# Differential keys and queries split straight out of PSUM, and a list scheduler that does not book the shared port ahead

## The chip, the core and the metric

The kernel runs on one core of a Trainium2 chip. The metric is device time in microseconds of one execution. A core has five engines that run in order and meet by semaphores: TensorE (PE; its weight loads are listed apart as PEld), VectorE (DVE), ScalarE (ACT), GpSimd (POOL) and SyncE (SP), which here issues all DMA transfers. TensorE reads SBUF and writes PSUM; POOL works in SBUF only.

## The reference

One decoder layer, sequence 512, model width 1024, all float32. Two attention branches share one input projection; the change touches the first.

```python
h = rmsnorm(x, ln_mix_g)
dq, dk, dv, nq, kc, vc, ksl, vsl, kwn, vwn, ng, mg = split(h @ w_in)
# differential attention: 8 heads, each with two query/key components c of 64, values of 128
dq, dk = rope(rmsnorm(dq)), rope(rmsnorm(dk))
s = einsum('bqhcd,bkhcd->bhcqk', dq, dk) * 64 ** -0.5
p = softmax(causal(s));  a = p[:, :, 0] - lam * p[:, :, 1]
y_diff = rmsnorm(a @ dv, subln_g) * (1 - lambda_init)
# sparse attention (NSA): 16 query heads, 4 key groups: compressed, selected and window branch
y_nsa = nsa_attention(...)
x = x + (sig(mg0) * (y_diff @ w_proj_diff) + sig(mg1) * (y_nsa @ w_proj_nsa)) @ w_out
x = x + relu(rmsnorm(x) @ w_mlp_up) ** 2 @ w_mlp_down
```

## The kernel before

Float32 products are made of rounded parts. Each operand is split into a high part (the value rounded to the matmul's format) and a low part (the rest): `split` makes a cast on ACT or DVE and a subtraction on DVE, or, for weights, on DVE or POOL. A projection is then three matmuls (high x high, high x low, low x high). Weights come in 157 pieces of up to 512 KB (`WStream`): wraw is the raw piece, whi and wlo its parts, each made in two halves of 512 columns, ahead of use.

The program goes through these stages: the norm of x and its transposes (hTh, hTl); the chunks of the input projection in four PSUM banks gb; beside them, as side streams, rope on the projected rows (`rope_stream`: t1r and t2r are its products, rw the roped rows), scores and softmax (`score_stream`), and probability times values (`value_stream`); the two output projections, merged by gates (tm, big) and w_out; and the MLP. The side streams end with the merge, some 650 to 725 us into the span. The first 77 weight pieces are used up before it.

Roped rows are transposed by TensorE into a PSUM bank ptp, one of two banks that all transposes share: keys (dk) or queries (dq) of one differential head, components 0 and 1 on the lower and the upper 64 partitions. `q_stacks` makes of a query bank two tiles of 128 partitions, qa and qb: high part on one half, low part on the other. `k_dups` makes of a key bank the tile kp (high and low, one buffer), and four DMAs copy it into kk, so that each component's parts lie on both halves. `scores` needs two matmuls then: query stack times doubled high keys, query stack times doubled low keys. The NSA keys (nk) go through `k_dups` as well. Tags: kk has 3 buffers, q has 9.

The order of all work is made before the launch. `Pe` interleaves the streams by an estimate of TensorE's time, and every instruction is noted with its priority, which is its place there (15 places ahead for the side streams). `Sched.flush` then makes a list schedule over ACT, DVE, POOL, PE and SP with prices per instruction (`price`), delays between engines and buffer counts, and issues the instructions in order of their start. Some instructions may go to either of two engines. `ported` says which instructions need the SBUF port that DVE and POOL are taken to share; self.port is the time until which it is taken. Before, an instruction under 64 elements needs none, and an engine that finds only port users ready books the one of highest priority from self.port on.

All instructions are recorded by one helper (line 357), so tiles tell them apart, not lines.

Of the kernel before, what the change touches and what calls it, by code (L numbers as in the profile page):

```python
# [11 lines left out]
F32 = mybir.dt.float32  # L12
# [119 lines left out]
class Sched:  # L132
# [34 lines left out]
    def price(self, eng, method, aps, k):  # L167
        if "accum_out" in k:
            aps = [x for x in aps if x is not k["accum_out"]]
        n = max(self.size(x) for x in aps)  # L170
        psum = any(self.tiles[x.tensor.name].space == "PSUM" for x in aps if x.tensor.name in self.tiles)
        if eng == "PE":
            if method == "transpose":
                return 113.0
            return max(113.0, 5.5 + self.size(aps[-1]) * 0.4315)
        if eng == "ACT":
            return (51 if psum else 93) + n * 0.8333 + (93 if "accum_out" in k else 0) + (
                93 if any(self.size(x) == 1 for x in aps[1:]) and n > 1 else 0)
        if eng == "DVE":
            ptr = sum(1 for x in aps[1:] if self.size(x) == 1) if n > 1 else 0  # L180
            if method in ("tensor_scalar", "tensor_copy") and not psum:
                return 69 + n * 0.52 + 61 * ptr
            if method == "memset":
                return 8 + n * 1.04
            if method == "reciprocal":
                return 69 + n * 6.25
            return 69 + n * 1.042 + 61 * ptr
        if eng == "POOL":
            if k.get("op") == OP.pow:
                return 300 + n * 165.0  # L190
            return 150 + n * 2.1
        return 20.0
# [2 lines left out]

    def ported(self, eng, method, aps, k):

        if max(self.size(x) for x in aps) < 64:
            return False
        if eng == "POOL":  # L200
            return k.get("op") != OP.pow
        return eng == "DVE" and method in self.TWICE and not any(
            self.tiles[x.tensor.name].space == "PSUM" for x in aps if x.tensor.name in self.tiles)

# [67 lines left out]
    def flush(self):  # L272

        ops, self.ops = self.ops, []
        self.wait = {e: [] for e in self.free}
        ok = {e: [] for e in self.free}
        fresh, again = [], set()
        for op in ops:
            for b in op.bufs:
                if b.group is None or b in again:  # L280
                    continue
                again.add(b)
                if b.granted:
                    self.held[b.group] += 1
                else:
                    fresh.append(b)
        for b in fresh:
            self.held.setdefault(b.group, 0)
            self.queue.setdefault(b.group, []).append(b)
        for op in ops:  # L290
            op.left, op.ready = 1, 0.0
            for d in op.deps:
                if d.left == -1:
                    op.ready = max(op.ready, d.end + self.lat(d.eng, op.eng, op.deps[d]))
                else:
                    d.users.append(op)
                    op.left += 1
            for b in op.bufs:
                if not b.granted:
                    b.waiting.append(op)  # L300
                    op.left += 1
        for g in list(self.queue):
            self.grant(g, 0.0)
        for op in ops:
            self.arm(op)
        done = []
        while len(done) < len(ops):
            best = None
            for e in self.free:
                for h, k in ((self.wait[e], 2), (ok[e], 1)):  # L310
                    while h and h[0][k].left == -1:
                        heapq.heappop(h)
                t = self.free[e] if ok[e] else max(self.free[e], self.wait[e][0][0]) if self.wait[e] else None
                if t is not None and (best is None or t < best[0]):
                    best = (t, e)
            assert best is not None, "no instruction can go on"
            t, e = best
            while self.wait[e] and self.wait[e][0][0] <= t:
                _, p, op = heapq.heappop(self.wait[e])
                if op.left == 0:  # L320
                    heapq.heappush(ok[e], (p, op))
            p, op = heapq.heappop(ok[e])
            if op.port[e] and self.port > t:
                put_off = [(p, op)]
                while ok[e] and put_off[-1][1].port[e]:
                    z = heapq.heappop(ok[e])
                    if z[1].left == 0:
                        put_off.append(z)
                if not put_off[-1][1].port[e]:
                    p, op = put_off.pop()  # L330
                else:
                    p, op = put_off.pop(0)
                for z in put_off:
                    heapq.heappush(ok[e], z)
            op.eng = e
            op.start = max(t, self.port) if op.port[e] else t
            op.end = op.start + op.ways[e][1]
            if op.port[e]:
                self.port = op.end
            self.free[e] = op.end  # L340
            if op.dma:
                self.hw = max(op.end, self.hw) + op.dma[0]
                self.dma = max(self.hw + 650, self.dma) + op.dma[1]
                op.end = self.dma
            op.left = -1
            done.append(op)
            for u in op.users:
                u.ready = max(u.ready, op.end + self.lat(e, u.eng, u.deps[op]))
                self.arm(u)
            for b in op.bufs:  # L350
                b.left -= 1
                b.end = max(b.end, op.end)
                if b.left == 0 and b.group is not None:
                    self.held[b.group] -= 1
                    self.grant(b.group, b.end + 150)
        for op in sorted(done, key=lambda o: o.start):
            op.ways[op.eng][0](*op.a, **op.k)  # L357
            op.ways = op.a = op.k = op.users = op.deps = None
# [68 lines left out]
def hybrid_block(ctx: ExitStack, tc: tile.TileContext, x, ln_mix_g, w_in, dqg, dkg, lq1, lk1, lq2, lk2,  # L427
# [137 lines left out]
    with ExitStack() as ps:  # L565
# [312 lines left out]
        def q_stacks(pt):  # L878
# [5 lines left out]
            V.tensor_tensor(qb[0:64], pt[64:128], f(qb[64:128]), op=OP.subtract)  # L884
            return qa, qb

        group_keys = {}

        def k_dups(pt, key):

            kp = att.tile([128, 2, 512], F32R, tag="kp", bufs=1, name="kp")
            split(kp[:, 0, :], kp[:, 1, :], pt)
            if key[0] == "dk":
                kk = k_tile()
                dst = [kk[:, s] for s in range(2)]
            else:

                if key[2] == 0:
                    for s in range(2):
                        group_keys[key[1], s] = k_tile()  # L900
                dst = [group_keys[key[1], s][:, key[2]] for s in range(2)]
            for s in range(2):
                for d in range(2):
                    Q.dma_start(f(dst[s][d * 64:(d + 1) * 64]), f(kp[s * 64:(s + 1) * 64]))
            return dst

        jobs = []
# [1 line left out]
        def rope_stream():  # L909

            for _ in range(8):
# [5 lines left out]
                yield 3000  # L917
                for c0, what, key in pairs:
                    sl = k_slots if what == "k" else q_slots
                    n = 2 if what == "q" else 1 if key[0] == "dk" else 2 - 2 * key[2]  # L920
                    yield sl.can(n)
                    yield t_bank()
                    sl.take(n)
                    pt = tpair(raws, c0)
                    ready[key] = there(key)
                    ready[key].tiles = k_dups(pt, key) if what == "k" else q_stacks(pt)
                    ready[key].after(6500 if what == "k" else 3500)
                    t_use(2000 if what == "k" else 3000)
                    yield 0
                r_slots.give(4)  # L930

# [93 lines left out]
        def scores(q, kk, i):  # L1025
# [3 lines left out]
                mm(sb[:, :n], q[:, i * 128:(i + 1) * 128], kk[:, z, :n], n, z == 0, z == 1)  # L1029
            return sb  # L1030

        def softmax_num(sb, i, stat):

            n = (i + 1) * 128
# [15 lines left out]
        def score_stream():  # L1050
            for h in range(8):
                yield there(("dk", h))
                yield there(("dq", h))
                kv, qv = ready["dk", h].tiles, ready["dq", h].tiles
                for i in reversed(range(NT)):
                    st = att.tile([128, 12], F32, tag="sm", bufs=8, name="sm")
                    n = (i + 1) * 128
# [2 lines left out]
                    ps_ = []  # L1060
                    for z in range(2):
                        yield s_bank()
                        ps_.append(softmax_num(scores(qv[z], kv[z], i), i, st[:, 2 * z:2 * z + 2]))
                        s_use(S_LAT + n)
                        yield 0
                    p0, p1 = ps_
# [4 lines left out]
                    probs["d", h, i] = p0  # L1071
                    stats[h, i] = st
                    there(("pd", h, i)).after(P_LAT + 3 * n)
                q_slots.give(2)
                k_slots.give(1)
            for p in range(2):
                for b in range(2):
# [571 lines left out]
```

## Time and profile before

| | |
|---|---|
| median of 3 runs | 1096.49 us (1095.57 to 1099.45) |
| the profiled execution | 1096.69 us, its span 1094.9 us |
| PE busy | 1053.8 us, 96% |
| DVE busy | 766.2 us, 70% |
| ACT busy | 465.6 us, 43% |
| POOL busy | 477.0 us, 44% |
| kk<-kp, the copies of the keys | 48 DMAs of 256 KB, 4.5 us to landing |

Matmuls are pipelined, so PE counts as busy also where it is slowed; a row's duration of a matmul is longer than the step from one to the next. A share of busy time is a mean over all stages, which have different limits. In a timeline the bracket behind a row gives the engine's idle time before it and what ended that. A wait for several semaphores is put down to the one that came last.

### The profile page before, as it was taken

The page shows a single profiled execution, that of the slowest core. Times are in us where ns is not written, and L with a number is a line of the kernel's source. Part 1 is how long each engine was busy: PE and PEld are TensorE (multiplying, and loading weights), DVE is VectorE, ACT ScalarE, POOL GpSimd, SP SyncE. Part 2 cuts the span into 40 slices and gives each one's busy share as a digit, 9 for nine tenths or more (in the row PEclk, how much of TensorE's full clock was granted, in tenths as well). Part 3 has the DMA queues.
Part 4 walks back from the last instruction along what each step waited for, and adds up shares of the span by engine and source line. Part 5 has one row for each costly group of instructions (what it writes and reads, how often), then busy time and mean ns, then how long its engine had stood idle before and what let it go on. Part 6 is the DMA issues. An engine that isn't in the chain of part 4 may idle for free.

```text
span 1094.9 us, 15737 instructions
## 1 busy us (share of the span) xinstructions
PE 1053.8 (96%) x5257; PEld 875.6 (80%) x5257; DVE 766.2 (70%) x1905; ACT 465.6 (43%) x1136; POOL 477.0 (44%) x475
## 2 busy tenths in 40 slices
PE   6999988899999999999999998999999999999998
PEld 5877867788787888887788886788888888888886
DVE  6779678899988999999989898556533323354232
ACT  4257335656464466665456563214222111242110
POOL 3745698348767372292212024423333222333221
PEclk9999988999999999999999999999999999999999
DMA  6362534642654224536363255622322223332232
GB/s 209 97 173 63 153 102 120 163 132 71 172 143 142 64 78 137 142 125 214 129 193 112 92 161 170 208 85 94 96 97 97 97 96 96 97 97 96 97 136 75
DMA packets 83616, 134.66 MB, mean 123 GB/s; under 512 B 8784, under 2 KB 33872, under 8 KB 83536
## 3 DMA queue, kind: packets, MB, share of 16 engines
q1 hardware_dynamic: 83536, 133.67, 39.7%
q8 instruction: 41, 0.67, 0.3%
q14 instruction: 39, 0.32, 0.1%
HBM read 106.64 MB, written 14.42 MB: 111 GB/s over the span
## 4 chain that ended last, share of the span: by engine, by line
PE 74%; DVE 12%; DMA 6%; POOL 4%; issue 2%; SPq 1%; ACT 1%; DVEq 0%; POOLq 0%; ACTq 0%
PE gb L357 38%; PE ga L357 22%; PE sb L357 4%; PE avn L357 4%; PE ptn L357 3%; DMA kk<-kp 3%; DVE p L357 2%; POOL str L357 1%; PE av L357 1%; POOL wlo L357 1%; SPq L357 1%; POOL t1r L357 1%; DVE al L357 1%; DVE sm L357 1%; DMA kk<-in_x_dram 1%
## 5 line engine op out<-in xcount | busy, mean ns | idle before, releaser
L357 POOL TENSOR_TENSOR wlo<-wraw,whi 128x512 fp32r<-128x512 f32 x203 | 289.0, 1432 | 522.7 <-ACT whi L357 396.2
L357 ACT CAST whi<-wraw 128x512 fp32r<-128x512 f32 (+2 forms) x217 | 130.0, 618 | 343.7 <-PE gb L357 167.0
L357 DVE CAST whi<-wraw 128x512 fp32r<-128x512 f32 x97 | 47.5, 489 | 199.7 <-PE ga L357 95.8
L357 PE MATMUL gb<-wlo,hTh 128*128 128x512 f32 (+2 forms) x352 | 136.0, 388 | 4.4 <-POOL wlo L357 2.4
L357 PE MATMUL gb<-whi,hTl 128*128 128x512 f32 (+2 forms) x352 | 135.0, 384 | 0.0
L357 PE MATMUL gb<-whi,hTh 128*128 128x512 f32 (+2 forms) x352 | 133.4, 388 | 1.5 <-ACT hTh L357 1.3
L357 DVE CUSTOM_DVE_ANT_0 p<-sb,cst 128x512 f32<-128x512 f32 (+2 forms) x192 | 92.1, 481 | 13.1 <-PE sb L357 11.7
L357 DVE TENSOR_TENSOR wlo<-wraw,whi 128x512 fp32r<-128x512 f32 (+1 forms) x111 | 92.2, 832 | 7.2 <-ACT whi L357 2.7
L357 ACT ACTIVATE p<-p,smn 128x512 f32<-128x512 f32 (+3 forms) x128 | 72.0, 563 | 26.6 <-DVE smn L357 26.2
L357 PEld LDWEIGHTS gb<-wlo,hTh 128*128 128x128 f32 x352 | 67.7, 192 | 14.8 <-POOL wlo L357 3.4
L357 PEld LDWEIGHTS gb<-whi,hTh 128*128 128x128 f32 x352 | 66.7, 191 | 11.5 <-ACT hTh L357 1.7
L357 PEld LDWEIGHTS gb<-whi,hTl 128*128 128x128 f32 x352 | 67.6, 192 | 10.3 <-DVE hTl L357 0.3
L357 DVE TENSOR_SCALAR p<-p,smn,gates 128x512 f32<-128x512 f32 (+3 forms) x128 | 66.9, 527 | 1.0
L357 PE MATMUL gb<-big,whi 128*128 128x512 f32 x192 | 65.1, 403 | 0.0
L357 PE MATMUL gb<-hTl,whi 128*128 128x512 f32 x160 | 64.7, 404 | 0.0
L357 PE MATMUL gb<-hTh,wlo 128*128 128x512 f32 x160 | 64.5, 403 | 0.0
L357 PE MATMUL gb<-hTh,whi 128*128 128x512 f32 x160 | 64.0, 400 | 0.0
L357 DVE TENSOR_TENSOR al<-ptn,ah 128x128 fp32r<-128x128 f32 (+3 forms) x128 | 61.3, 482 | 3.6 <-ACT ah L357 2.0
L357 PE MATMUL ga<-h2l,whi 128*128 128x512 f32 x160 | 62.5, 391 | 0.0
L357 PE MATMUL ga<-h2h,whi 128*128 128x512 f32 x160 | 62.4, 391 | 0.0
L357 PE MATMUL ga<-h2h,wlo 128*128 128x512 f32 x160 | 62.3, 390 | 0.0
L357 ACT CAST ah<-ptn 128x384 fp32r<-128x384 f32 (+3 forms) x98 | 41.2, 424 | 49.1 <-PE ptn L357 38.1
(248 smaller groups left out, 2634.7 us busy)
## 6 DMA issues: line engine op xcount, KB each, us to landing
wraw<-in_w_in_dram SPq DMA_DIRECT2D x36, 512.0 KB, 3.6
wraw<-in_w_mlp_up_dram SPq DMA_DIRECT2D x32, 512.0 KB, 3.8
wraw<-in_w_mlp_down_dram SPq DMA_DIRECT2D x32, 512.0 KB, 3.5
kk<-kp SPq DMA_DIRECT2D x48, 256.0 KB, 4.5
wraw<-in_w_in_dram SPq DMA_DIRECT2D x36, 256.0 KB, 3.2
big<-yd SPq DMA_DIRECT2D x16, 512.0 KB, 3.4
yd<-yo SPq DMA_DIRECT2D x8, 512.0 KB, 3.3
wraw<-in_w_proj_diff_dram SPq DMA_DIRECT2D x8, 512.0 KB, 4.3
```

What stands on the lines that cost most here:

```text
L357: op.ways[op.eng][0](*op.a, **op.k)
```

## The change

For the differential heads, `dk_stacks` writes each key component's high part to its own half and its low part to the other half, straight out of PSUM. `dq_stacks` writes the queries' high parts to both halves of the same kk tile, and the low parts to a tile ql, each component on its own half. `diff_scores` takes two matmuls: the query's high part on both halves times high and low keys (128 partitions), and the query's low part times the high keys (64 partitions). The product of both low parts is left out. `k_dups`, now for NSA keys alone, splits into the own half and copies it to the other by one DMA for each component. kp is gone; a differential head takes one q buffer for two.

In the scheduler, DVE instructions under 64 elements count as port users too; a one-column scalar_tensor_tensor costs more in `price`; and an engine that finds only port users ready, with the port taken, issues none and looks again when the port is free or its next instruction is ready.

```diff
         if eng == "DVE":
-            ptr = sum(1 for x in aps[1:] if self.size(x) == 1) if n > 1 else 0
+            ptr = sum(1 for x in aps[1:] if self.size(x) == 1) if n > 1 else method == "scalar_tensor_tensor"
...
     def ported(self, eng, method, aps, k):
-        if max(self.size(x) for x in aps) < 64:
-            return False
         if eng == "POOL":
-            return k.get("op") != OP.pow
+            return k.get("op") != OP.pow and max(self.size(x) for x in aps) >= 64
         return eng == "DVE" and method in self.TWICE and not any(
...
-                if not put_off[-1][1].port[e]:
+                go = not put_off[-1][1].port[e]
+                if go:
                     p, op = put_off.pop()
-                else:
-                    p, op = put_off.pop(0)
                 for z in put_off:
                     heapq.heappush(ok[e], z)
+                if not go:
+                    self.free[e] = min(self.port, self.wait[e][0][0]) if self.wait[e] else self.port
+                    continue
             op.eng = e
-            op.start = max(t, self.port) if op.port[e] else t
+            op.start = t
...
+        def dk_stacks(pt):
+            kt = k_tile().rearrange("p a b n -> p (a b) n")
+            for s in range(2):
+                own, other = slice(s * 64, s * 64 + 64), slice(64 - s * 64, 128 - s * 64)
+                copy(kt[own, s], pt[own])
+                V.tensor_tensor(kt[other, s], pt[own], f(kt[own, s]), op=OP.subtract)
+            return kt
+
+        def dq_stacks(pt, kt):
+            ql = att.tile([128, 512], F32R, tag="q", bufs=9, name="ql")
+            for s in range(2):
+                own, other = slice(s * 64, s * 64 + 64), slice(64 - s * 64, 128 - s * 64)
+                copy(kt[own, 2 + s], pt[own])
+                A.copy(kt[other, 2 + s], pt[own])
+                V.tensor_tensor(ql[own], pt[own], f(kt[own, 2 + s]), op=OP.subtract)
+            return ql
...
         def k_dups(pt, key):
-            kp = att.tile([128, 2, 512], F32R, tag="kp", bufs=1, name="kp")
-            split(kp[:, 0, :], kp[:, 1, :], pt)
...
             for s in range(2):
-                for d in range(2):
-                    Q.dma_start(f(dst[s][d * 64:(d + 1) * 64]), f(kp[s * 64:(s + 1) * 64]))
+                own, other = slice(s * 64, s * 64 + 64), slice(64 - s * 64, 128 - s * 64)
+                split(dst[s][own, 0], dst[s][own, 1], pt[own])
+                Q.dma_start(f(dst[s][other]), f(dst[s][own]))
...
+        def diff_scores(kt, ql, z, i):
+            n = (i + 1) * 128
+            own = slice(z * 64, z * 64 + 64)
+            sb = pscore.tile([128, 512], F32, tag="s", name="sb")
+            mm(sb[:, :n], kt[:, 2 + z, i * 128:(i + 1) * 128], kt[:, z, :n], n, True, False)
+            mm(sb[:, :n], ql[own, i * 128:(i + 1) * 128], kt[own, z, :n], n, False, True)
+            return sb
...
-                        ps_.append(softmax_num(scores(qv[z], kv[z], i), i, st[:, 2 * z:2 * z + 2]))
+                        ps_.append(softmax_num(diff_scores(kt, ql, z, i), i, st[:, 2 * z:2 * z + 2]))
```

The streams' estimate of when a key is ready changes with it: 3500 ns after its transposes for differential keys, which was 6500, and 6500 still for NSA keys.

What the scheduler makes of it is seen in the order of the built programs. The first place is DVE's row in the projection of differential heads 4 and 5, around 188 to 200 us of the trace of before; ptp is the transposed bank, sb a score bank, sm statistics, ISA p,sm the score maximum. Before, the cast into kp stands behind four DMA queues (DMAHW):

```order
L357 TENSOR_TENSOR qa_515<-ptp_514,qa_515 64x512 [waits PE_49,Activation_49]
L357 TENSOR_TENSOR qb_516<-ptp_514,qb_516 64x512
L357 RECIPROCAL sm_519<-sm_519 128x4 [waits Activation_49]
L357 TENSOR_SCALAR ys_358<-yt_541,sm_466 128x128 [waits Pool_49]
L357 SCALAR_TENSOR_TENSOR sm_519<-sm_519,lam_149 128x1 [waits DVE_49]
L357 ISA p_544,sm_533<-sb_543,cst_129 128x384 [waits PE_49]
L357 ISA sm_533 128x1
L357 SCALAR_TENSOR_TENSOR p_524<-p_532,sm_519,p_524 128x512 [waits DVE_49]
L357 CAST kp_521<-ptp_520 128x512 [waits DMAHW3_49,DMAHW4_49,DMAHW2_49,DMAHW1_49]
L357 ISA p_556,sm_533<-sb_555,cst_129 128x384 [waits PE_49]
L357 ISA sm_533 128x1
L357 TENSOR_TENSOR kp_521<-ptp_520,kp_521 128x512 [waits DVE_49]
```

The same heads in the changed program:

```order
L357 CAST kk_515<-ptp_514 64x512 [waits PE_49]
L357 ISA p_522,sm_520<-sb_521,cst_129 128x384 [waits PE_49]
L357 ISA sm_520 128x1
L357 TENSOR_TENSOR kk_515<-ptp_514,kk_515 64x512 [waits DVE_49]
L357 RECIPROCAL sm_508<-sm_508 128x4 [waits Activation_49]
L357 TENSOR_TENSOR yt_537<-yt_537,av_536 128x128 [waits Activation_49]
L357 ISA p_528,sm_520<-sb_527,cst_129 128x384 [waits PE_49]
L357 ISA sm_520 128x1
L357 CAST kk_515<-ptp_514 64x512
L357 COPY hs_575<-hb_496 128x130 [waits PE_49]
L357 TENSOR_TENSOR kk_515<-ptp_514,kk_515 64x512 [waits DVE_49]
```

The DMA queues are gone from the waits, and one head's key takes four instructions out of its bank where it took two.

The second place is DVE's row in the merge, around 664 to 672 us of before; tm are the gated sums, kk here their split, big the NSA output's split. Before:

```order
L357 TENSOR_TENSOR big_1027<-yp_1990,big_1027 128x512 [waits Activation_49]
L357 SCALAR_TENSOR_TENSOR tm_2051<-tm_2051,gb_1978 128x512 [waits DMAHW3_49,PE_49]
L357 SCALAR_TENSOR_TENSOR tm_2054<-tm_2054,gb_1979 128x512 [waits DMAHW0_49,PE_49]
L357 CAST whi_2047<-wraw_2036 128x512 [waits DMAHW1_49,PE_49,Pool_49]
L357 TENSOR_TENSOR tm_2055<-tm_2055,tm_2054 128x512 [waits DMAHW7_49,DMAHW3_49,DVE_49]
L357 SCALAR_TENSOR_TENSOR kk_2053<-tm_2052,kk_2053 128x512 [waits Activation_49]
L357 SCALAR_TENSOR_TENSOR kk_2053<-tm_2055,kk_2053 128x512 [waits Activation_49]
```

In the changed program:

```order
L357 TENSOR_TENSOR big_1009<-yp_1970,big_1009 128x512 [waits Activation_49]
L357 SCALAR_TENSOR_TENSOR tm_2031<-tm_2031,gb_1958 128x512 [waits DMAHW4_49,PE_49]
L357 TENSOR_TENSOR big_1009<-yr_2030,big_1009 128x512 [waits DMAHW5_49,Activation_49]
L357 TENSOR_TENSOR tm_2032<-tm_2032,tm_2031 128x512 [waits DMAHW1_49,DVE_49]
L357 CAST whi_2027<-wraw_2016 128x512 [waits DMAHW1_49,PE_49]
L357 SCALAR_TENSOR_TENSOR tm_2034<-tm_2034,gb_1959 128x512 [waits DMAHW7_49,DMAHW3_49]
L357 TENSOR_TENSOR wlo_2028<-wraw_2016,whi_2027 128x512 [waits PE_49,Activation_49]
L357 SCALAR_TENSOR_TENSOR kk_2033<-tm_2032,kk_2033 128x512 [waits Activation_49]
```

DVE now makes the first sum tm<-tm itself, which POOL made before, and a wlo between. Over the merge DVE makes 7 of the 8 such sums, where it made 3.

The third place is PE's row at one of the first score pairs, among matmuls of the projection (gb). Before:

```order
L357 MATMUL gb_244<-hTh_68,whi_218 128x512
L357 MATMUL sb_228<-kk_214,qa_216 128x512 [waits DMAHW3_49,DMAHW2_49]
L357 MATMUL sb_228<-kk_214,qa_216 128x512
L357 MATMUL gb_244<-hTl_69,whi_218 128x512
L357 MATMUL gb_244<-hTh_68,wlo_219 128x512
```

In the changed program, where the second of the pair is the one on 64 partitions:

```order
L357 MATMUL gb_243<-hTl_69,whi_216 128x512
L357 MATMUL sb_251<-kk_213 128x384 [waits DVE_49]
L357 MATMUL sb_251<-kk_213,ql_215 128x384
L357 MATMUL gb_243<-hTh_68,wlo_217 128x512
L357 MATMUL gb_244<-hTh_68,whi_216 128x512
```

There are 64 such matmuls from ql, and no two of them stand next to each other.

## Rows read from the trace of the kernel before

**Rows 1.** Windows by stage: busy us (instructions) per engine, granted clock, DMA, GB/s.

```profile
28.00:150.00 122.00, 119.78 (x603) 99.66 (x604) 93.98 (x223) 58.02 (x143) 77.83 (x83) 1.00 0.40 113
150.00:210.00 60.00, 50.13 (x249) 40.65 (x247) 49.20 (x120) 31.49 (x78) 39.30 (x46) 0.86 0.57 149
210.00:650.00 440.00, 429.31 (x2394) 361.77 (x2393) 408.17 (x1197) 260.21 (x708) 206.72 (x241) 1.00 0.44 132
650.00:725.00 75.00, 69.88 (x306) 56.10 (x305) 49.73 (x69) 22.26 (x40) 30.12 (x19) 0.98 0.48 162
725.00:1094.90 369.90, 366.02 (x1629) 302.54 (x1628) 145.49 (x249) 80.28 (x142) 114.07 (x74) 1.00 0.30 97
sum 1094.90, PE 1053.82 PEld 875.65 DVE 766.17 ACT 465.57 POOL 476.97; mean PE 175.64 PEld 145.94 DVE 127.70 ACT 77.60 POOL 79.49
```

**Rows 2.** Chain of waits, the MLP: start us, us, what.

```profile
873.43 43.52 PE ga L357 x192
```

**Rows 3.** Waits on the copies of kp: us in total, times, longest us.

```profile
ACT kp L357 <- DMA kk<-kp: 5.7, 3, 2.1
DVE kp L357 <- DMA kk<-kp: 5.7, 3, 2.8
```

**Rows 4.** Timeline of PE, waits at scores: start us, us, instruction [idle before].

```profile
71.83 0.73 PE L357 MATMUL sb<-kk,qb 128*128 128x512 f32 x2 [1.06 <-DVE sm L357]
...
199.84 0.50 PE L357 MATMUL sb<-kk,qa 128*128 128x256 f32 x2 [2.40 <-DVE sm L357]
...
291.24 0.70 PE L357 MATMUL sb<-kk,qb 128*128 128x512 f32 x2 [1.26 <-DVE sm L357]
```

**Rows 5.** Timeline of DVE, 198 us: the second head's kp.

```profile
198.62 0.69 DVE L357 CAST kp<-ptp 128x512 fp32r<-128x512 f32 x1 [2.84 <-DMA kk<-kp]
```

**Rows 6.** Timeline of PE, other waits.

```profile
157.46 0.70 PE L357 MATMUL ptp<-cst,rw 128*128 128x128 f32 x4 [2.76 <-DVE kp L357]
...
175.65 0.80 PE L357 MATMUL gb<-wlo,hTh 128*128 128x512 f32 x1 [1.82 <-DVE wlo L357]
...
673.31 0.80 PE L357 MATMUL ga<-big,whi 128*128 128x512 f32 x1 [3.29 <-DVE big L357]
...
708.13 0.50 PE L357 MATMUL ga<-whi,kk 128*128 128x512 f32 x1 [1.35 <-DVE tm L357]
```

**Rows 7.** Timeline of DVE and POOL, 173 us.

```profile
173.77 1.22 DVE L357 SCALAR_TENSOR_TENSOR sm<-sm,lam 128x1 f32<-128x1 f32 x1
...
173.21 1.76 POOL L357 TENSOR_TENSOR wlo<-wraw,whi 128x512 fp32r<-128x512 f32 x1
```

**Rows 8.** Timeline of POOL and DVE in the merge.

```profile
667.75 3.15 POOL L357 TENSOR_TENSOR wlo<-wraw,whi 128x512 fp32r<-128x512 f32 x2
...
668.00 1.77 DVE L357 TENSOR_TENSOR tm<-tm 128x512 f32<-128x512 f32 x1
```

**Rows 9.** By form (busy us, mean ns | idle before); by tile (ns min/median/max).

```profile
L357 DVE TENSOR_TENSOR wlo<-wraw,whi 128x512 fp32r<-128x512 f32 x110 | 91.7, 834 | 7.2 <-ACT whi L357 2.7 <-issue 0.4
...
L357 DVE TENSOR_TENSOR qa<-ptp,qa 64x512 fp32r<-64x512 f32 x16 | 10.9, 684 | 0.9 <-ACT qb L357 0.5
...
L357 ACT CAST qb<-ptp 64x512 fp32r<-64x512 f32 x15 | 8.7, 581 | 0.8 <-DVE qa L357 0.6
...
L357 DVE TENSOR_TENSOR wlo<-wraw,whi x111: 568/693/1782, 9.2 to 1080.7; 128x512 fp32r<-128x512 f32 x110, 128x400 fp32r<-128x400 f32 x1
...
L357 DVE TENSOR_TENSOR t2r<-rw,ropes x47: 211/284/837, 37.7 to 342.8; 128x128 f32<-128x128 f32 x36, 128x64 f32<-128x64 f32 x6, 128x256 f32<-128x256 f32 x5
L357 DVE TENSOR_TENSOR rw<-t1r,str x32: 399/684/1822, 42.8 to 495.5; 128x512 f32<-128x512 f32 x24, 128x256 f32<-128x256 f32 x8
...
L357 DVE SCALAR_TENSOR_TENSOR sm<-sm,lam x32: 204/211/1234, 75.0 to 328.5; 128x1 f32<-128x1 f32 x32
```

**Rows 10.** The costliest groups: a matmul's and a weight load's mean ns.

```profile
L357 PEld LDWEIGHTS gb<-wlo,hTh 128*128 128x128 f32 x352 | 67.7, 192 | 14.8 <-POOL wlo L357 3.4
...
L357 PE MATMUL ga<-h2l,whi 128*128 128x512 f32 x160 | 62.5, 391 | 0.0
```

More of the change, by code (lines that the diff above doesn't have):

```diff
@@ L885, in q_stacks @@
             return qa, qb
+        def dk_stacks(pt):
[13 more added lines that the diff above has]
+            return ql
         group_keys = {}
         def k_dups(pt, key):
-            kp = att.tile([128, 2, 512], F32R, tag="kp", bufs=1, name="kp")
-            split(kp[:, 0, :], kp[:, 1, :], pt)
[L893 to L901, printed above, removed]
+            if key[2] == 0:
+                for s in range(2):
+                    group_keys[key[1], s] = k_tile()
+            dst = [group_keys[key[1], s][:, key[2]] for s in range(2)]
             for s in range(2):
-                for d in range(2):
-                    Q.dma_start(f(dst[s][d * 64:(d + 1) * 64]), f(kp[s * 64:(s + 1) * 64]))
+                own, other = slice(s * 64, s * 64 + 64), slice(64 - s * 64, 128 - s * 64)
+                split(dst[s][own, 0], dst[s][own, 1], pt[own])
+                Q.dma_start(f(dst[s][other]), f(dst[s][own]))
             return dst
@@ L919, in rope_stream @@
                     sl = k_slots if what == "k" else q_slots
-                    n = 2 if what == "q" else 1 if key[0] == "dk" else 2 - 2 * key[2]
+                    n = {"dq": 1, "dk": 1, "nq": 2}.get(key[0]) or 2 - 2 * key[2]
                     yield sl.can(n)
@@ L925, in rope_stream @@
                     ready[key] = there(key)
-                    ready[key].tiles = k_dups(pt, key) if what == "k" else q_stacks(pt)
-                    ready[key].after(6500 if what == "k" else 3500)
-                    t_use(2000 if what == "k" else 3000)
+                    if key[0] == "dk":
+                        ready[key].tiles = dk_stacks(pt)
+                    elif key[0] == "dq":
+                        ready[key].tiles = dq_stacks(pt, ready["dk", key[1]].tiles)
+                    else:
+                        ready[key].tiles = k_dups(pt, key) if what == "k" else q_stacks(pt)
+                    ready[key].after(6500 if key[0] == "nk" else 3500)
+                    t_use(2000 if key[0] == "nk" else 3000)
                     yield 0
@@ L1053, in score_stream @@
                 yield there(("dq", h))
-                kv, qv = ready["dk", h].tiles, ready["dq", h].tiles
+                kt, ql = ready["dk", h].tiles, ready["dq", h].tiles
                 for i in reversed(range(NT)):
@@ L1073, in score_stream @@
                     there(("pd", h, i)).after(P_LAT + 3 * n)
-                q_slots.give(2)
+                q_slots.give(1)
                 k_slots.give(1)
```

## Prediction

> **What bounds the kernel now.** I read the windows of busy time first, since a mean over the whole program hides its stages. From 725 us on TensorE is never idle inside the stretch: 366.0 us busy of 369.9, the rest the last output's way out, and DVE at 145.5 us has ample room [rows 1]. There the chain of waits is nothing but matmuls, 192 of 128x512 in 43.52 us, 226.7 ns from start to start [rows 2]. Nothing done to DVE, ACT or POOL can shorten that stage. The time that can be won is ahead of it. Counted as length minus PE busy, TensorE idles 2.2 us in 28 to 150, 9.9 in 150 to 210, 10.7 in 210 to 650 and 5.1 in 650 to 725 [rows 1]: 27.9 us. To this comes the clock: the granted clock is 0.86 in 150 to 210 and 0.98 in 650 to 725 [rows 1], so stretches at the lower level (1.2 instead of 2.4 GHz) behind the waits cost 60 x 0.14 = 8.4 us and 75 x 0.02 = 1.5 us of work. So some 38 us, 3.5% of the program, is about all that a better order can win; a worse one has no such limit.
>
> In those stages DVE is the busy one: 94.0 of 122, 49.2 of 60, 408.2 of 440 us [rows 1]. Engines run in order, so one DVE instruction that stands still holds up everything behind it. Two kinds of standing still are in the rows.
>
> First, the single buffer kp. Its next writer must wait until four DMAs have read it. ACT and DVE waited six times for that, 5.7 us each in total [rows 3]. At 198.62 a DVE cast into kp had waited 2.84 us [rows 5]; a score maximum stands behind it, and TensorE idled 2.40 us for the bank that this frees. TensorE waits of the same origin are at 71.83 (1.06) and 291.24 (1.26) [rows 4].
>
> Second, DVE and POOL in each other's way. At 173.77 a scalar_tensor_tensor of one column, whose median is 211 ns, took 1.22 us [rows 7, 9], and ended as a POOL wlo did that had begun at 173.21 and took 1.76; the wlo that TensorE needed stood behind it, and TensorE idled 1.82 us [rows 6]. At 668.00 a DVE add took 1.77 us beside two POOL wlo of 3.15 us [rows 8]; more of the same follow until 673.31, where TensorE had idled 3.29 us [rows 6]. In sum: the 110 wlo of 512 columns on DVE have a mean of 834 ns and a median of 693, which is 110 x 0.141 = 15.5 us of standing [rows 9].
>
> **The change, part by part.** I sum against the profiled execution: 1096.7 us, of which 1094.9 is the span [rows 1]; the median of the runs is 1096.5, the same within 0.2.
>
> *Keys without kp.* 48 DMAs kk<-kp become 8, and the kp buffer goes. The DVE place in the order shows it: the cast that waited for four DMA queues is now one that waits for its transposes alone; behind it stand the score maximum and the bank of TensorE, as before. The idle to be had is 1.06 + 2.40 + 1.26 = 4.7 us, and of the 8.4 us of lower clock a share by idle length (2.40 of 2.40 + 2.76 + 1.82 = 6.98), 2.9 us: 7.6 us. A new order will meet some other wait there, so I take -6 (bounds 0 and -7.6). The 40 DMA issues that leave SP move weight loads earlier; TensorE waits for weights only through wlo, so I count nothing more.
>
> *What replaces it.* Each of 8 dk tiles has two casts and two subtractions where it had one of each, each of 8 dq tiles four casts for two, each of 4 NSA keys one cast and one subtraction more. That is 12 subtractions on DVE at 684 ns = 8.2 us, and 28 casts, mostly on ACT at 581 ns = 16 us [rows 9]. ACT has the room (465.6 us busy of 1094.9 [rows 1]). What can hurt is that the PSUM bank of the transposes, one of two, is held longer: by one cast and one subtraction, or two casts, some 1.2 us each on 16 tiles, 19 us if TensorE stood for all of it, 0 if the weight matmuls between cover it. Transposes stand among weight matmuls in the order, so I take +1.
>
> *Half-height matmuls.* The second score matmul of the 64 differential pairs now reads ql and its key on 64 partitions instead of 128. Columns stay, so by themselves they save nothing; they could gain only if two of them stood side by side on different halves, and in the order none does. Each stands between full-height matmuls: 128 changes of height. No row before shows such a matmul. Bounds: 0, if the stream goes on at 226.7 ns; from above, a standstill until the matmul ahead has ended and the next weights are in: 391 - 227 = 164 ns [rows 2, 10], plus 192 ns of weight load [rows 10], 356 ns, x 128 = 45.6 us. I take +4, near the lower end, since weight loads and matmuls overlap throughout (PE 1053.8 and PEld 875.7 us busy in a span of 1094.9 [rows 1]), and since part would fall where TensorE waits anyway. Here the Trainium skill speaks against the change: TensorEngine Tiling (Array Packing), section Tiling Modes, Key Properties, says that changing the tiling mode, not just the tile, drains TensorE. No run here has shown that yet. By that rule each change costs at least the 164 ns, 21 us in all.
>
> *The scheduler.* Small DVE instructions count as port users, and an engine that finds the port taken no longer books the next turn but looks again later. Ties go to DVE, which stands ahead of POOL in the scheduler's list of engines. The order shows how much this moves: of 311 wlo of 512 columns POOL had 201 and DVE 110; now it is 110 and 201. In the 77 weight pieces before the merge, DVE goes from 44 to 70 wlo, and it takes over 46 pieces of the rope products and sums as well; the rest of the move lies later, where DVE has 224 idle us. So before the merge DVE gets 26 x 0.693 = 18 us of wlo, 46 x some 0.37 = 17 us of rope (between the 284 ns of a t2r and the 684 of a full-width piece [rows 9]) and the 8.2 us above, 43 us, and has 122 + 60 + 440 - 551.4 = 70.6 us idle to put them in. Against that, POOL loses the same 26 wlo and 46 rope pieces, and DVE with them a good part of its standing (15.5 us in wlo alone, over the whole program). I take these two as even, +1, with bounds -5 and +15 (a third of the 43 us landing on TensorE's path).
>
> What is won shows where TensorE waited for the port: 2.76 at 157.46 (behind a chain of small DVE and POOL instructions), 1.82, 3.29, and 1.35 at 708.13 [rows 6] = 9.2 us, with the rest of the lower clock, 5.5 + 1.5: 16.2 us. In the merge stage the order takes 7 of 8 tm additions to DVE and leaves POOL little to collide with, so I trust that 3.29 and 1.35 most go; in 150 to 180 us everything is reordered, and waits move as easily as they vanish. I take half: -8 (bounds 0 and -16).
>
> Sum: -6 + 1 + 4 + 1 - 8 = -8: 1096.7 - 8 = 1088.7, on the median's footing 1088.5. I say 1088.
>
> **The rivals.** (a) *Change of height drains TensorE.* For: nothing in the trace contradicts it, and 128 places is many. Against: TensorE is not the last to arrive everywhere in 60 to 330 us. The other terms sum to -12, so it decides from 12 / 128 = 94 ns a change; at 164 ns it is 21 - 12 = +9: 1106, and with exposed weight loads more. Slower. (b) *The waits only move.* DVE before the merge carries 43 us more; if that eats what the port and kp give back, the time is 1097. For it: DVE is at 89% there. (c) *The order really gets good:* kp and port groups go whole (-7.6 and -16), half of the remaining idle of 210 to 650 too (-4.7), and changes of height cost nothing: 1096.7 - 28 = 1068. For it: each of the long waits has a cause that the change names.
>
> **How the numbers follow.** Forecast 0.42, its own range 1080 to 1095; (a) 0.19 around 1106; (b) 0.20 around 1097; (c) 0.19 around 1068. About 0.5% (5.5 us) is what a measurement here can tell from no change: faster means below 1091.0, slower above 1102.0. Some 0.09 of the forecast lies above 1091, and a little of (b) below it. Faster: 0.33 + 0.19 + 0.02 = 0.54; same: 0.09 + 0.17 = 0.26; slower: 0.19 + 0.01 = 0.20. The range that leaves 2 in 10 out is 1067 to 1107.
>
> **What would show it.** Right: no wait for a DMA into keys before the merge other than the NSA keys'; the clock at full level in 150 to 210; POOL well under 400 us busy with DVE's wlo mean nearer 693 ns; no 3 us gap in the merge; PE busy in the last 370 us unchanged. Wrong: matmuls sb<-kk,ql whose followers start 150 ns or more late, 64 times over, with PE idle or stretched in 60 to 330 us (a); DVE busy at 95% before the merge and TensorE waiting for al, p and wlo (b); a bank wait of ptp for casts into kk (the longer hold).

## The result and the profile after

The changed kernel takes 1112.89 us (median of 4 runs, 1108.86 to 1113.26) against 1096.9 us before: a ratio of 1.0136, 95% interval 1.0117 to 1.0154. It is slower by some 16 us where 8 us less were forecast, and lies above the range. The profiled execution took 1112.71 us, its span 1110.9 us, 16.0 us more than before.

The windows by stage answer to [rows 1]; columns as there.

```profile
28.00:150.00 122.00, 120.71 (x585) 96.28 (x584) 95.80 (x248) 59.68 (x144) 48.39 (x55) 1.00 0.32 96
150.00:210.00 60.00, 56.46 (x245) 42.06 (x244) 51.35 (x136) 35.32 (x85) 35.20 (x40) 0.89 0.26 77
210.00:650.00 440.00, 427.72 (x2329) 352.55 (x2328) 405.83 (x1226) 253.23 (x688) 173.61 (x198) 0.99 0.38 114
650.00:725.00 75.00, 71.69 (x328) 58.62 (x327) 54.72 (x108) 28.67 (x58) 9.89 (x7) 0.98 0.59 193
725.00:1110.90 385.90, 381.17 (x1696) 315.08 (x1694) 180.46 (x310) 83.36 (x147) 27.42 (x21) 1.00 0.31 97
```

In 28 to 150 us TensorE is busier than before (120.71 against 119.78 us) and yet made 585 matmuls where it had made 603; in 150 to 210 it was busy for 56.46 us with 245 where it had needed 50.13 for 249. An engine that is busier and gets less done is being slowed, not starved. Past the merge the pace is as before: the chain of waits shows the same 192 matmuls of the MLP in the same 43.52 us, 15.1 us later [rows 2]; start us, us, what:

```profile
888.52 43.52 PE ga L357 x192
```

So 15.1 of the 16.0 us are lost ahead of these matmuls. The timeline of PE shows one pair of score matmuls, the second of which has 64 partitions (start us, us, instruction):

```profile
85.72 0.28 PE L357 MATMUL av<-vt,al 128*128 128x256 f32 x1
85.83 0.33 PE L357 MATMUL sb<-kk 128*128 128x384 f32 x1
86.10 0.43 PE L357 MATMUL sb<-kk,ql 64*128 64x384 f32 x1
86.46 0.50 PE L357 MATMUL gb<-hTl,whi 128*128 128x512 f32 x1
86.80 0.39 PE L357 MATMUL gb<-hTh,wlo 128*128 128x512 f32 x1
87.03 0.40 PE L357 MATMUL gb<-hTh,whi 128*128 128x512 f32 x1
```

and the timeline of PEld its weight loads:

```profile
85.72 0.19 PEld L357 LDWEIGHTS sb<-kk 128*128 128x128 f32 x1
86.10 0.18 PEld L357 LDWEIGHTS sb<-kk,ql 64*128 64x128 f32 x1 [0.19 <-issue]
86.46 0.19 PEld L357 LDWEIGHTS gb<-hTl,whi 128*128 128x128 f32 x1 [0.18 <-issue]
86.57 0.19 PEld L357 LDWEIGHTS gb<-hTh,wlo 128*128 128x128 f32 x1
86.80 0.19 PEld L357 LDWEIGHTS gb<-hTh,whi 128*128 128x128 f32 x1
```

Read the two side by side. The load for the matmul at 87.03 starts at 86.80, with the matmul ahead, and is done before its own begins. The load for the half-height matmul starts at 86.10, with its own matmul, and so does the one for the full-height matmul behind it, at 86.46: at each change of height the load no longer lies beside the matmul ahead. This holds for all 128 changes in the trace: there a load starts 3 ns or less ahead of its matmul, elsewhere a median of 223 ns ahead. The load behind a change is late too: the one at 86.57 starts 0.11 us after the matmul ahead instead of with it, and its matmul comes as much too late. So each change stretches two steps, the one that leads to it and the one behind it; the step out of the half-height matmul is both. A step of 384 columns most often takes 174 ns and one of 512 takes 227. Here 85.83 to 86.10 is 96 ns too long, 86.10 to 86.46 is 186 too long and 86.46 to 86.80 is 113 too long: 395 ns for two changes.

Over all 64 places, leaving out steps before which the engine stood idle 60 ns or more, the mean surplus is 114 ns into the half-height matmul, 188 out of it and 100 in the step behind: 7.3 + 11.8 + 6.4 = 25.5 us. The surplus of all other steps went from 25.9 to 24.5 us, and that of the steps left out, which stand behind idle times, from 37.6 to 28.4 us: an engine that comes later waits less. 25.5 - 1.4 - 9.2 = 14.9 of the 16.0 us; the last 1.1 us I did not trace. The group of these loads, by form (busy us, mean ns | idle before, releaser), shows the same: the weight loader stood idle 10.2 us before them with no releaser that the profile shows ("issue"):

```profile
L357 PEld LDWEIGHTS sb<-kk,ql 64*128 64x128 f32 x64 | 11.9, 186 | 12.7 <-issue 10.2
```

### The profile page after: what moved, and what is told of

It is laid out like the page before. It is cut to its first block, busy times and chain, and to the rows that moved or that the text cites. A ratio compares the mean times of both kernels' runs of the same rounds, so it can differ in the third digit from the quotient of the medians.

```text
span 1110.9 us, 15583 instructions
## 1 busy us (share of the span) xinstructions
PE 1076.9 (97%) x5257; PEld 880.5 (79%) x5257; DVE 807.9 (73%) x2077; ACT 473.7 (43%) x1146; POOL 300.7 (27%) x333
## 4 chain that ended last, share of the span: by engine, by line
PE 76%; DVE 15%; DMA 3%; POOL 2%; issue 2%; ACT 1%; SPq 0%; DVEq 0%; ACTq 0%; POOLq 0%
PE gb L357 40%; PE ga L357 21%; PE sb L357 5%; PE avn L357 3%; DVE p L357 3%; PE ptn L357 3%; PE av L357 2%; PE hb L357 1%; DVE wlo L357 1%; DMA big<-yd 1%; DVE kk L357 1%; DVE t1r L357 1%; DVE rw L357 1%; DVE al L357 1%; POOL str L357 1%
## 5 line engine op out<-in xcount | busy, mean ns | idle before, releaser
L357 POOL TENSOR_TENSOR wlo<-wraw,whi 128x512 fp32r<-128x512 f32 (+1 forms) x111 | 149.2, 1356 | 616.5 <-DVE whi L357 404.6
L357 ACT CAST whi<-wraw 128x512 fp32r<-128x512 f32 x206 | 123.5, 617 | 351.1 <-PE gb L357 182.5
L357 DVE TENSOR_TENSOR wlo<-wraw,whi 128x512 fp32r<-128x512 f32 x203 | 141.5, 727 | 4.7 <-ACT whi L357 0.2
L357 PE MATMUL gb<-big,whi 128*128 128x512 f32 x192 | 68.3, 416 | 1.3 <-DMA big<-yd 1.3
L357 ACT CAST ah<-ptn 128x128 fp32r<-128x128 f32 (+3 forms) x94 | 39.7, 423 | 52.9 <-PE ptn L357 40.4
L357 DVE TENSOR_SCALAR p<-p,smn,gates 128x512 f32<-128x512 f32 (+3 forms) x128 | 61.0, 485 | 1.1
```

## The experiments

Three theories. T1: the loss is the change between 128 and 64 partitions on TensorE. T2: it is the scheduler, which loads DVE with POOL's work. T3: the added casts and subtractions hold PSUM banks longer.

**The scheduler's three edits alone, on the kernel before.** The diff is the change's diff up to `dk_stacks`: the price, the port rule and the look-again rule. Later the first two are taken together as the port edit.

> The kernel before with the three scheduler edits alone; keys and queries as before (kp, 48 DMAs, all matmuls on 128 partitions). T1 (the loss is the change between 128 and 64 partitions on TensorE, some 150 ns a change, 19 us in all, and the scheduler gains a little): 1085 to 1096 us, PE excess between matmuls no larger than before. T2 (the loss is the scheduler, which loads DVE with POOL's wlo): 1105 to 1115 us, with TensorE waiting for DVE in 28 to 650 us.

Measured: 1106.48 us, ratio 1.0097 (1.0083 to 1.0111), 10.1 us slower. T2 predicted this, T1 did not; how far one such order can be trusted is tested at the end of this section. The waits of this kernel (us in total, times, longest) show where some of it went:

```profile
ACT kp L357 <- DMA kk<-kp: 8.8, 2, 4.4
DVE kp L357 <- DMA kk<-kp: 8.4, 3, 2.9
...
PE ptc L357 <- DVE kp L357: 3.5, 1, 3.5
```

Waits for the copies of kp rose from 5.7 + 5.7 us [rows 3] to 8.8 + 8.4, and one of them held TensorE for 3.5 us. So a new order can meet the same buffer at a worse moment.

**The keys and queries alone, with the old scheduler.** The other half of the diff.

> The changed kernel with the old scheduler: new keys and queries alone, with the half-height matmuls. T1 (change of height): 1105 to 1117 us, 64 matmuls sb<-kk,ql that start late and whose followers start late, some 300 ns a pair. T2 (scheduler): 1090 to 1098 us. T3 (the loss is the PSUM bank held longer by more casts): also slow, so this run does not tell T1 from T3; the full-height run does.

Measured: 1114.24 us, 1.0155 (1.013 to 1.0179). As slow as the whole change without any edit of the scheduler, so T2 alone can't be the cause.

**Full height.** The low queries get one tile of 128 partitions per head.

```diff
-            ql = att.tile([128, 512], F32R, tag="q", bufs=9, name="ql")
+            ql = [att.tile([128, 512], F32R, tag="q", bufs=9, name="ql") for _ in range(2)]
...
-                V.tensor_tensor(ql[own], pt[own], f(kt[own, 2 + s]), op=OP.subtract)
+                V.tensor_tensor(ql[s][own], pt[own], f(kt[own, 2 + s]), op=OP.subtract)
+                A.copy(ql[s][other].rearrange("p (b n) -> p b n", b=8),
+                       zz[other, None, :].to_broadcast([64, 8, 64]))
...
-            mm(sb[:, :n], ql[own, i * 128:(i + 1) * 128], kt[own, z, :n], n, False, True)
+            mm(sb[:, :n], ql[z][:, i * 128:(i + 1) * 128], kt[:, z, :n], n, False, True)
```

> The changed kernel, but the low queries are one 128-partition tile per head with zeros in the other half, so that all matmuls are 128 partitions high; this adds 16 ACT copies and a second query slot, and the result is the same. T1: the 19 us go, 1090 to 1097 us. T2 and T3 (scheduler, or casts and PSUM banks): 1110 to 1116 us, no better than the changed kernel, since the same work stands on DVE and more on ACT.

Measured: 1096.37 us, 1.0001 (0.9993 to 1.001). The 16.5 us are gone although ACT has 16 copies more and DVE the same work. That speaks for T1 and against T2 and T3, though the order of the instructions moves with this edit as well.

**Half height in the kernel before.** Nothing else changes: the order of every engine is that of before, instruction for instruction.

```diff
-        def scores(q, kk, i):
+        def scores(q, kk, i, half=(0, 0)):
...
-                mm(sb[:, :n], q[:, i * 128:(i + 1) * 128], kk[:, z, :n], n, z == 0, z == 1)
+                h = slice(half[z] * 64, 128)
+                mm(sb[:, :n], q[h, i * 128:(i + 1) * 128], kk[h, z, :n], n, z == 0, z == 1)
...
-                        ps_.append(softmax_num(scores(qv[z], kv[z], i), i, st[:, 2 * z:2 * z + 2]))
+                        ps_.append(softmax_num(scores(qv[z], kv[z], i, (0, 1)), i, st[:, 2 * z:2 * z + 2]))
```

> The kernel before, with one edit: the second score matmul of each of the 64 differential pairs reads only partitions 64 to 127 of the query and key, which leaves out half of that product. The instructions and their order are the same on every engine; only 128 changes of height are new. T1: 1112 to 1117 us if most of 128 x 150 ns = 19 us lands on the path, at least 1106. T2 and T3: 1097 us, no difference.

Measured: 1110.86 us, 1.0137 (1.0123 to 1.0151): 14.5 us, 13.5 to 16.6 by the interval. This is the cleanest of the runs, since half the contracted rows cost more time than all of them in one and the same order. The same stretch of PE, before:

```profile
236.03 0.39 PE L357 MATMUL sb<-kk,qa 128*128 128x512 f32 x1
236.26 0.22 PE L357 MATMUL ob<-w2s,gh 128*128 128x128 f32 x1
236.32 0.44 PE L357 MATMUL sb<-kk,qa 128*128 128x512 f32 x1
236.60 0.40 PE L357 MATMUL gb<-whi,hTh 128*128 128x512 f32 x1
236.84 0.22 PE L357 MATMUL ob<-w2s,gh 128*128 128x128 f32 x1
```

and with the half-height matmul:

```profile
245.76 0.39 PE L357 MATMUL sb<-kk,qa 128*128 128x512 f32 x1
245.99 0.22 PE L357 MATMUL ob<-w2s,gh 128*128 128x128 f32 x1
246.14 0.49 PE L357 MATMUL sb<-kk,qa 64*128 64x512 f32 x1
246.56 0.50 PE L357 MATMUL gb<-whi,hTh 128*128 128x512 f32 x1
246.90 0.22 PE L357 MATMUL ob<-w2s,gh 128*128 128x128 f32 x1
```

From the first ob to the second it took 0.58 us, now 0.91. Over the 64 pairs the surplus is 109 + 190 + 105 ns, 25.6 us in all; other steps give back 2.9 us and the steps behind idle times 7.9 us, which leaves 14.8, and the span grew by 15.0. So of about 200 ns for each change some 115 arrive at the end.

**Both matmuls of a pair at half height.** Twice the half-height matmuls, about the same number of changes (`(1, 1)` for `(0, 1)` in the line above): in 58 of the 64 pairs the two stand next to each other in TensorE's order, in 6 another matmul lies between, which makes 140 changes for 128.

> The kernel before with both score matmuls of each differential pair on partitions 64 to 127 alone, which leaves out half of the differential scores' products. Twice as many half-height matmuls as in the run with one of them, but the same 128 changes between 128 and 64 partitions. T1a (the cost is per change of height): the same as with one half-height matmul, 1109 to 1113 us. T1b (the cost is per half-height matmul, such as a slower weight load): 1122 to 1128 us. T2: 1097 us.

Measured: 1110.79 us, 1.0134 (1.0112 to 1.0156), the same as with one. The price is on the change, not on the matmul (T1a). In the timeline of PE the row with x2 holds both matmuls of the pair:

```profile
218.24 0.40 PE L357 MATMUL gb<-wlo,hTh 128*128 128x512 f32 x1
218.57 0.73 PE L357 MATMUL sb<-kk,qa 64*128 64x512 f32 x2
219.23 0.50 PE L357 MATMUL gb<-whi,hTl 128*128 128x512 f32 x1
219.56 0.40 PE L357 MATMUL gb<-whi,hTh 128*128 128x512 f32 x1
```

218.24 to 219.56 is 1.32 us for four steps of 227 ns: 0.41 too long, for two changes as before. Over the 58 pairs the step between the two matmuls is 95 ns too long and the step out of the second 94 ns: apart, they are what the 190 ns out of a lone one hold together.

**Full height with the old scheduler.**

> The changed kernel with low queries of full height (zeros in the other half) and with the old scheduler: the new keys alone, without kp and without changes of height. What is measured so far: the scheduler alone +10.1 us on the kernel before, full height with the new scheduler 0.0, both on record. T1 with a scheduler that costs the same +10 everywhere: 1086 us. T1 with a scheduler whose cost came from the kp buffer only (it runs later into the DMAs that read kp): 1092 to 1100 us, near the full-height run with the new scheduler. T3 (casts and banks cost): above 1097 us.

Measured: 1101.07 us, 1.0038 (1.0025 to 1.005). The keys without kp gained nothing in this order. That is above what T1 gave for either kind of scheduler (1086, and 1092 to 1100) and within T3's "above 1097"; nudged orders of the same rules, below, took 1097.45 and 1089.95, so this one time decides nothing for T3. Against the run with the keys alone it is 13.2 us faster: the changes of height once more.

**The scheduler's two edits apart, at full height**, and each with other parts of the change.

> The full-height kernel with one of the scheduler's two edits: an engine that finds the port taken looks again later and books nothing, but small DVE instructions don't count as port users and the old price of scalar_tensor_tensor stands. If the move of wlo from POOL to DVE comes from the look-again rule (ties go to DVE) DVE has about 200 of them here, as in the changed kernel. If this edit is the one that costs, it is slower than the full-height run without it; if the small instructions are what gains, this one lacks it: 1097 to 1105 us. If neither edit matters once kp is gone: 1093 to 1099 us.

Measured: 1101.57 us, 1.0043 (1.0021 to 1.0064): nothing against the old scheduler. DVE made 206 wlo, against 117 with the old scheduler, so it is the look-again rule that moves them from POOL.

> The full-height kernel with the other scheduler edit: small DVE instructions count as port users, scalar_tensor_tensor of one column has the new price, and a taken port is still booked ahead. If counting the small instructions is what gains, this is the best one: 1086 to 1093 us. If the gain and the loss lie in the look-again rule, it is near the full-height run with the old scheduler. If neither edit matters once kp is gone: 1093 to 1099 us.

Measured: 1084.52 us, 0.9889 (0.9869 to 0.991). This is faster than both kernels, and than the one before by 12 us. DVE made 106 wlo.

> The kernel before with the port edit alone: small DVE instructions count as port users, a taken port is still booked ahead; keys through kp as before, all matmuls 128 partitions high. With the new keys at full height this edit was worth -16.6 us (1101.1 to 1084.5). If its worth does not hang on the keys: 1080 to 1086 us. If the kp buffer spoils it, as it spoiled the whole scheduler edit (+10.1): 1092 to 1102 us, with waits for the DMAs that read kp.

Measured: 1095.84 us, 0.9996 (0.9985 to 1.0007): on the old keys the edit is worth nothing.

> The changed kernel without the look-again rule: new keys with half-height matmuls, and the port edit. Against the best run so far (1084.5 us, the same with full-height low queries) it has only the 128 changes of height more. T1: +14 to +18 us as in the other pairs of runs, 1098 to 1103 us. If a better order leaves the cost of the changes more exposed: up to 128 x 150 ns = 19 us, 1104 us. T2: 1085 us.

Measured: 1097.85 us, 1.0017 (1.0006 to 1.0027): 13.3 us above the run with full height (T1 had said 14 to 18), so the price of the height is nearly the same in a third order.

> The full-height kernel with both scheduler edits (1096.4 us), and POOL ahead of DVE in the scheduler's list of engines, so that a tie at the end of a port booking goes to POOL. If the look-again rule costs because its ties hand wlo to DVE: POOL has about 200 wlo again or more, DVE's busy time falls back to some 770 us, and the time to 1083 to 1090 us. If the loss lies in the look-again rule's order itself and not in who gets the wlo: 1093 to 1100 us.

```diff
-        self.free = {e: 0.0 for e in ("PE", "ACT", "DVE", "POOL", "SP")}
+        self.free = {e: 0.0 for e in ("PE", "ACT", "POOL", "DVE", "SP")}
```

Measured: 1096.98 us, 1.0001 (0.9989 to 1.0013). Its page, against that of the full-height run with DVE first:

```profile
PE 1054.1 (96%) x5257; PEld 873.2 (80%) x5257; DVE 675.4 (62%) x1823; ACT 481.4 (44%) x1164; POOL 575.9 (53%) x585
```

```profile
PE 1053.5 (96%) x5257; PEld 871.7 (80%) x5257; DVE 807.4 (74%) x2066; ACT 483.9 (44%) x1167; POOL 304.0 (28%) x339
```

132 us of DVE's work went to POOL and the time did not move. Who makes the wlo is not what decides; this guess of mine fell.

**Is the scheduler's part a mechanism at all?** Its worth so far was +10.1, -1.4 and -4.7 us for both edits, -0.6, -16.4 and -16.6 for the port edit. So I changed one unrelated number of the scheduler's model by a few ns, at full height, which reorders much of the program, and timed each rule again.

```diff
-           ("DVE", "PE"): 362,
+           ("DVE", "PE"): 370,
```

> The best run (full height, port edit alone, 1084.5 us) with one unrelated number of the scheduler changed: 370 ns instead of 362 for the way from DVE to TensorE. M (the port edit's -16.6 us is a mechanism): 1081 to 1088 us. S (it is scatter of the order): anywhere from 1084 to 1103 us, most likely above 1090.

> The full-height kernel with the old scheduler (1101.1 us) and the same 370 for 362 ns. M: 1098 to 1104 us. S: 1084 to 1103 us, most likely below 1097.

> The full-height kernel with both scheduler edits and 370 for 362 ns from DVE to TensorE. M: 1094 to 1099 us, as the two orders so far. S: 1084 to 1101 us.

```diff
-    OWN = {"ACT": 142, "DVE": 127, "POOL": 102}
+    OWN = {"ACT": 142, "DVE": 130, "POOL": 102}
```

> The best run (1084.5 us) with another unrelated number changed: 130 ns instead of 127 for DVE's own latency. M: 1081 to 1088 us. S: 1084 to 1103 us, most likely above 1090.

> The full-height kernel with the old scheduler and 130 for 127 ns of DVE's own latency. M (the rules differ in mean, old slowest): 1097 to 1102 us. S (all rules share one scatter): 1084 to 1101 us, as likely below 1094 as above.

> The full-height kernel with both scheduler edits (1096.4 us) and the same 130 for 127 ns. M: 1093 to 1099 us. S: 1084 to 1103 us, off by more than 4 us either way.

```diff
-           ("POOL", "PE"): 300,
+           ("POOL", "PE"): 330,
```

> The full-height kernel with the port edit alone and 330 for 300 ns from POOL to TensorE. M: below 1095 us as the three orders so far. S: 1084 to 1101 us.

Measured, medians in us, all at full height:

| rules | as is | 370 | 130 | 330 | mean |
|---|---|---|---|---|---|
| old | 1101.07 | 1097.45 | 1089.95 | | 1096.2 |
| port edit alone | 1084.52 | 1094.53 | 1091.91 | 1088.81 | 1089.9 |
| both edits | 1096.37 | 1092.21 | 1096.83 | | 1095.1 |

Under one rule a nudge of 3 to 30 ns moves the time by up to 11 us (old: 1101.07 to 1089.95). All seven times lie in the ranges of S (scatter of the order) and two in those of M (a mechanism); S also said that both edits at 130 would move by more than 4 us, and they moved by 0.5. For the sizes S is right: the -16.6 us of the port edit were partly a bad draw of the old order and a good one of its own. The means put the port edit first by 6 us, with a standard error of about 4 (spread of the rows, three and four orders), which is not clear of the scatter; both edits against none is -1 and can't be told from nothing. What, if anything, the look-again rule costs stays open. The kernel before was timed in one order only.

## Why the prediction was wrong, by its steps

**The step that failed is the term for half-height matmuls: +4 us, measured +13.2 to +16.5** in four comparisons: 14.5 in one order, 13.2, 13.3 and 16.5 between orders that also carry scatter. The bounds of 0 to 45.6 us held it. The choice near the lower end did not: I argued from loads and matmuls that overlap throughout [rows 1], but this overlap is just what a change of height takes away, so it could not be called on as cover. The price of about 200 ns lies between the 164 ns of the standstill [rows 2, 10] and the 356 ns with the load on top, near the 192 ns of a weight load [rows 10]. The second argument, that part falls where TensorE waits anyway, was right: 8 to 9 of 25.5 us did. Here I had weighed and put aside a rule of the Trainium skill, TensorEngine Tiling (Array Packing), section Tiling Modes, Key Properties: changing the tiling mode drains TensorE. The trace agrees as far as it goes: at all 128 changes the load starts only with its matmul. That the array itself is empty then, or that 64 rows count as another mode, can't be read from it: the ends of matmuls are modelled, and it lists active rows, not modes.

**Rival (a) is what happened,** by its mechanism. It said slower from 94 ns a change; net of what idle times give back, the experiment in one order has 14.5 / 128 = 113. Its sign is there too: the matmul behind the half-height one is late in all 64 places, by 143 ns or more, and by over 150 in 51. Its number, 1106 and with exposed loads more, comes near 1112.9 partly by luck: it counted 21 us for the changes, of which about 15 reached the end, and -12 for the rest, which did not come.

**The other terms were over-sized: -12 us forecast, none measured** at full height (1096.37 against 1096.36; over three orders -1.4, with one order of before and a scatter that would hide a few us). The port edit alone did reach -12 in one order (1084.52), but its four orders average 1089.9. At full height the clock and the waits of 150 to 210 us did get better, and 210 to 650 us got worse; the windows of that run, columns as in [rows 1]:

```profile
150.00:210.00 60.00, 53.84 (x284) 42.80 (x284) 57.00 (x158) 43.12 (x107) 36.31 (x42) 0.97 0.26 79
210.00:650.00 440.00, 425.46 (x2366) 355.06 (x2365) 411.45 (x1240) 257.61 (x698) 171.43 (x197) 1.00 0.39 120
```

TensorE's idle time fell from 9.9 to 6.2 us in the first and rose from 10.7 to 14.5 in the second; in surplus of steps, idle ones included, the first won 7.8 us and the second lost 7.0. Term by term:

- Keys, -6: the waits for copies of kp are gone, and no DMA into keys holds anything ahead of the merge. Yet with the old scheduler three orders average what before took (1096.2 against 1096.4). So the waits moved, and that part of rival (b) holds.
- Longer hold of the PSUM bank, +1: small, as forecast. In the trace after TensorE waited 0.33 us for a cast into kk (one wait, at 108.21 us), 0.9 us for qb before transposes (two) and 0.2 us for ql (one).
- Scheduler, -8: POOL fell to 300.7 us and DVE's wlo to a mean of 731 ns (834 before [rows 9]), as expected. By form, busy us, mean ns | idle before:

```profile
L357 DVE TENSOR_TENSOR wlo<-wraw,whi 128x512 fp32r<-128x512 f32 x201 | 140.7, 731 | 4.7 <-ACT whi L357 0.2
```

  The 3.29 us wait of the merge [rows 6] became two shorter ones, while the clock in 150 to 210 us stayed at 0.89 (0.86 before), not full; at full height it was 0.97. The timeline of PE, waits in brackets:

```profile
173.96 0.90 PE L357 MATMUL pta<-cst,p 128*128 128x128 f32 x3 [1.40 <-DVE yo L357]
...
687.64 0.50 PE L357 MATMUL ga<-big,whi 128*128 128x512 f32 x1 [1.15 <-DVE big L357]
...
695.30 0.50 PE L357 MATMUL ga<-big,whi 128*128 128x512 f32 x1 [1.93 <-DVE big L357]
```

- DVE's load, +1 with rival (b)'s 95%: it is 405.83 of 440 us in 210 to 650, 92%, less than before. Not the cause; with 132 us taken off DVE the time was the same.

The error that carries both: I credited waits seen in one order to their causes, one by one. The nudges show that the time differs by up to 11 us between orders made by the same rule, so -12 us for all of them was more than one order could tell.

## What to carry to other kernels

Keep the height of neighbouring matmuls the same: 64 rows of zeros cost nothing in the stream here (1096.37 us against 1112.89), a lone matmul of 64 partitions between others of 128 costs some 0.4 us of it. Where a list schedule decides the order, time several nudged orders of each version before crediting an edit with less than 1%. Cover that comes from an overlap may only be counted if the edit leaves the overlap alone.

## What the runs showed of the hardware

A change between matmuls of 128 and 64 partitions took about 200 ns of TensorE's stream, half of it in the step that leads to it and half in the step behind (404 ns a pair of changes, mean over 64 pairs; by columns, medians from 301 ns at 128 to 471 at 256 in the kernel before with half height), and two half-height matmuls in a row paid it once. The weight load, 183 to 192 ns, started with its matmul there instead of ahead of it, and the next one 106 ns late. A DVE scalar_tensor_tensor of one column still took up to 1226 ns after the scheduler counted it as a port user (1234 before [rows 9]; median 214):

```profile
L357 DVE SCALAR_TENSOR_TENSOR sm<-sm,lam x32: 190/214/1226, 67.6 to 332.5; 128x1 f32<-128x1 f32 x32
```
